# The S5 generator of a four-branch mixer begins among the gate tiles, with longer pairs of steps

## The chip, the cores and the metric

The kernel runs on one core of one Trainium2 chip. The core's engines work side by side, each from its own queue in order: TensorE (PE, with its weight loads apart as PEld), VectorE (DVE), ScalarE (ACT), GpSimd (POOL), and SyncE (SP), which issues DMA transfers. The metric is the device time of one execution in microseconds (us).

## The reference, cut to what matters

Two layers, each over 256 context tokens and 1024 latent tokens of width 1024. One projection of the normed input feeds four mixers (latent attention, a diagonal S5 state space model, a gated linear recurrence, pooling), four gate paths and four sets of merge logits:

```python
def _merge(branches, gate_paths, merge_logits, w_branch, w_out):
    gp = jnp.split(gate_paths, N_BRANCH, axis=-1)
    ml = jnp.split(merge_logits, N_BRANCH, axis=-1)
    y = 0.0
    for n in range(N_BRANCH):
        y = y + jax.nn.sigmoid(ml[n]) * ((branches[n] * jax.nn.silu(gp[n])) @ w_branch[n])
    return y @ w_out
```

The S5 mixer has 16 groups with 64 complex states each, run over the tokens forwards and backwards; a readout gives back 16 channels per group, and a GLU with one 256x256 product follows.

In the first layer all 1280 tokens are produced, in the second the context is only read, so its output covers the 1024 latent tokens.

## The kernel before

Activations lie channels by tokens. The tokens are cut in three chunks, `CH = [(0, 256), (256, 512), (768, 512)]`; the first layer (0) works on all three where it makes outputs, the second (1) on the last two. A projection tile is one 128-column slice of `w_in`: `load_w` fetches it (`wr`) and splits it in a high and a low part (`wh` on ACT, `wl` on DVE, line 117), and `hgemm` runs 24 matmuls for each chunk into a PSUM tile `pg`, which has two buffers.

After the attention, `layer` issues in this order of the program: the six gate tiles that the pooling has left over (`gate`: three chunks each in layer 0, two in layer 1), the eight logit tiles of the pooling branch (`logits`), and `merge`, which goes through the branches in the order pooling, recurrence, attention, S5. The merge of the pooling branch is short: 6 matmuls `pm<-b,wph/wpl` for each tile and chunk, and one DVE instruction `y<-y,pm` that takes the result, since its logits are there already. The `pm` tiles have two buffers. The later branches compute their logit tile (24 matmuls) ahead of each such product.

The S5 work between them is a Python generator, `s5`, of eight pairs of groups. A pair first forms its matrices on DVE (`tm<-hao`, `er<-tm`, `wc<-tm`, `ph<-tm`), transposes them on PE (`pS<-ident,er`), then makes its state products (`pS<-u,wb`, copied to `rqx`), rotates them (`tm<-rqx,ph`, `er<-tm`), scans them (eight scans, lines 935 and 936, `rqx<-hkeep,er`), rotates back into `er`, and reads out on PE (`pS<-u,wk` and `pS<-er,wc`, copied to `yo`, stored to `yD`). The generator stops at `yield`:

```python
for _ in range(lead[0]):   # ahead of the state products
    yield
...
for _ in range(lead[1]):   # from the rotation back to the readout
    yield
...
yield                      # behind the readout
```

and after the pairs `s5_out` adds two stops for each chunk ahead of its GLU product (`pS<-rqx,er`). Each chunk of a logit tile calls `next(s5)` once, and so does each chunk of a merge tile of the second and third branch (`if bi > 0: ... next(s5, None)`); before the S5 branch's merge, `for _ in s5: pass` runs what is left.

The order of the program is not the order on the engines. A scheduler takes instructions by priority (their place in the program, earlier first, with `hp()` blocks put ahead) as soon as its own estimate says that their inputs are there, and writes one fixed order for each engine. So gate tiles fill the attention's gaps on PE, and the S5 pairs are taken up when the attention leaves PSUM (`pS`, three buffers shared) and DVE to them.

Of the kernel before, what the change touches and what calls it, by code (L numbers as in the profile page):

```python
# [36 lines left out]
MLA, S5B, LRUB, POOLB = 0, 1, 2, 3  # L37
# [26 lines left out]
class Net:  # L64
# [928 lines left out]
                self.dma(oD[f][:, s0:s0 + n], t)  # L993


    def gate(self, l, b, f, lat, gD):

        w = self.load_w(self.I["w_in"][l, 9 + 2 * b + f], NK)
        for ci in lat:
            s0, n = CH[ci]  # L1000
            ps = self.hgemm(w, ci)
            t = self.st(n)
            with self.hp():
                self.act(t, ps, AF.Tanh, scale=0.5)
                self.stt(t, t, 1.0, ps, ALU.add, ALU.mult)
                self.dma(gD[f][:, s0:s0 + n], t)

    def logits(self, l, b, j, lat, tD, bg):

        w = self.load_w(self.I["w_in"][l, 17 + 8 * b + j], NK)  # L1010
        for ci in lat:
            s0, n = CH[ci]
            ps = self.hgemm(w, ci)
            t = self.st(n)
            with self.hp():
                self.act(t, ps, AF.Tanh, scale=0.5)
                self.dma(tD[j][:, s0:s0 + n], t)
            next(bg, None)
# [105 lines left out]
    def layer(self, l, pre):  # L1124
        tc = self.tc
        lat = [0, 1, 2] if l < DEPTH - 1 else [1, 2]
        oD = {b: self.dram((2, 128, NT), "oD") for b in ORDER}
        gD = {b: self.dram((2, 128, NT), "gD") for b in ORDER}
        with self.phase("pr") as pr, self.phase("pa") as pa:
            m = self.mla_in(l, pa, pre)  # L1130
            pads = [self.lru_pad(pa, pre[2 + f]) for f in range(2)] if pre else None
            self.mla_kv(l, m, pa)
            uF, uD = self.s5_in(l, pr)
            xl = self.lru_in(l, pa, pads)
            self.lru(l, xl, oD[LRUB], lat, pa, pr)
            self.cq_in(l, m, lat, pa)
            self.mla_q(l, m, lat, pa)
            xp = self.pool_in(l, lat, pa)
            gates = ((b, f) for b in ORDER for f in range(2))
            for _ in self.pool(l, xp, oD[POOLB], lat, pa, pr):  # L1140
                b, f = next(gates)
                self.gate(l, b, f, lat, gD[b])
        with self.phase("p5") as p5:
            with self.phase("pt") as pt_:
                self.attention(m, lat, oD[MLA], pt_)
            for b, f in gates:
                self.gate(l, b, f, lat, gD[b])
            s5 = self.s5(l, uF, uD, oD[S5B], lat, p5, (2, 4) if len(lat) == 3 else (1, 3))
            tD = self.dram((NK, 128, NT), "tD")
            for j in range(NK):  # L1150
                self.logits(l, ORDER[0], j, lat, tD, s5)
            with self.phase("pc") as pc:
                self.merge(l, lat, oD, gD, tD, pc, s5)
# [269 lines left out]
```

## Time and profile before

| what | us |
|---|---|
| median of 3 runs (2327.64 to 2333.63) | 2330.84 |
| the profiled execution | 2328.08 |
| its span in the trace | 2326.3 |
| PE busy in it | 2267.7 |
| DVE busy in it | 1547.8 |
| ACT busy in it | 969.2 |

PE is the engine that counts: it has work nearly all the time. Its busy time takes in matmuls that overlap, so what it loses is read from its idle time in the waits and the timeline, and from the pace of matmuls (24 of a chunk in 5.6 us), not from the busy share. DVE's share is a mean over stages in which it is loaded very differently.

### The profile page before, as it was taken

Reading aid. Unit: us, or ns where it says so; the run is one execution under the profiler, and the core shown is the slowest. Engines: PE = TensorE matmul, PEld = TensorE weight load, DVE = VectorE, ACT = ScalarE, POOL = GpSimd, SP = SyncE. Lnnn points to the kernel's source line nnn. Section 1 sums busy time; section 2 is a strip of 40 time slices with the busy share of each in tenths; the row PEclk is TensorE's granted clock in tenths of the full one; section 3 lists DMA queues with packets and bytes.
Section 4 is the critical chain, followed back from the end, with each engine's and each line's share of the span. In section 5 each row is a group of like instructions: output and inputs, shape, how many; then the busy total and the mean of one; then the engine's idle time right before and its main releaser. Section 6 shows DMA issues by size and latency. Waiting matters only on the chain. (4 is left out here: it accounts for less than half of the span.)

```text
span 2326.3 us, 33035 instructions
## 1 busy us (share of the span) xinstructions
PE 2267.7 (97%) x11680; PEld 1848.0 (79%) x11680; DVE 1547.8 (67%) x3524; ACT 969.2 (42%) x1966; POOL 208.3 (9%) x261
## 2 busy tenths in 40 slices
PE   8899999999999999999999999999999999999999
PEld 3687878888788888788888787778888788877887
DVE  5664769676877888656455745688667978863243
ACT  4646656665312222312243445756664232322131
POOL 0000000000001111111112100000000011111100
PEclk9999999999999999999999999999999999999999
DMA  8141242211534223433234332242213431332134
GB/s 278 56 157 40 103 123 67 76 56 54 174 94 122 74 77 109 127 94 104 96 100 157 115 116 70 99 132 73 70 56 116 118 105 53 86 110 85 49 115 157
DMA packets 215750, 236.34 MB, mean 102 GB/s; under 512 B 78112, under 2 KB 141344, under 8 KB 215584
## 3 DMA queue, kind: packets, MB, share of 16 engines
q1 hardware_dynamic: 215072, 234.19, 32.4%
q8 instruction: 92, 1.51, 0.3%
q0 software_dynamic: 512, 0.03, 0.1%
q14 instruction: 74, 0.61, 0.1%
HBM read 175.70 MB, written 58.46 MB: 101 GB/s over the span
## 5 line engine op out<-in xcount | busy, mean ns | idle before, releaser
L135 PE MATMUL pg<-h,wh 128*128 128x512 f32 (+1 forms) x4608 | 1346.8, 374 | 0.2 <-DVE h L117 0.2
L135 PEld LDWEIGHTS pg<-h,wh 128*128 128x128 f32 x4608 | 828.7, 188 | 154.6 <-issue 4.5
L135 PE MATMUL pg<-h,wl 128*128 128x512 f32 (+2 forms) x2304 | 871.1, 378 | 1.8 <-DVE wl L117 1.6
L135 PEld LDWEIGHTS pg<-h,wl 128*128 128x128 f32 (+1 forms) x2304 | 434.0, 188 | 81.1 <-issue 3.6
L117 DVE TENSOR_TENSOR wl<-wr,wh 128x512 fp32r<-128x512 f32 x268 | 190.3, 712 | 172.0 <-ACT wh L132 171.1
L132 ACT ACTIVATE wh<-wr 128x512 fp32r<-128x512 f32 x268 | 167.9, 628 | 277.9 <-PE pg L135 150.8
L132 ACT ACTIVATE st<-pg 128x512 f32<-128x512 f32 (+1 forms) x200 | 110.4, 552 | 350.5 <-PE pg L135 343.1
L117 POOL TENSOR_TENSOR y<-y,st 128x512 f32<-128x512 f32 (+1 forms) x120 | 153.1, 1276 | 733.8 <-DVE st L120 696.3
L135 PE MATMUL pm<-b,wph 128*128 128x512 f32 (+1 forms) x640 | 184.4, 372 | 1.6 <-DVE b L117 1.6
L132 ACT ACTIVATE P<-pS,sm,qs 128x512 f32<-128x512 f32 (+1 forms) x200 | 138.6, 702 | 45.3 <-DVE sm L124 43.2
L135 PE MATMUL pS<-k,q 128*128 128x512 f32 (+1 forms) x600 | 145.4, 365 | 0.6 <-DVE q L117 0.4
L120 DVE SCALAR_TENSOR_TENSOR st<-st,pm 128x512 f32<-128x512 f32 (+1 forms) x120 | 75.5, 629 | 105.4 <-PE pm L135 104.9
L135 PEld LDWEIGHTS pm<-b,wph 128*128 128x128 f32 x640 | 115.7, 188 | 24.5 <-DVE b L117 3.1
L135 PE MATMUL pP<-pt,v 128*128 128x256 f32 x656 | 126.9, 301 | 3.4 <-DVE pt L117 1.2
L135 PEld LDWEIGHTS pP<-pt,v 128*128 128x128 f32 x656 | 99.1, 188 | 35.1 <-ACT pt L132 21.5
L117 DVE TENSOR_TENSOR pt<-pm,pt 128x512 fp32r<-128x512 f32 x164 | 107.0, 683 | 26.5 <-ACT pt L132 25.8
L135 PE MATMUL pm<-b,wpl 128*128 128x256 f32 (+1 forms) x320 | 120.1, 376 | 4.5 <-ACT b L132 2.6
L518 DVE TENSOR_REDUCE sm<-pS 128x1 f32<-128x512 f32 (+1 forms) x200 | 113.4, 587 | 14.3 <-PE pS L135 13.0
L132 ACT ACTIVATE pt<-pm 128x512 fp32r<-128x512 f32 x164 | 91.0, 600 | 70.5 <-PE pm L138 70.1
L135 PEld LDWEIGHTS pS<-k,q 128*128 128x128 f32 x600 | 98.7, 189 | 18.6 <-ACT P L132 4.8
L138 PE MATMUL pm<-ident,P 128*128 128x128 f32 x656 | 106.3, 274 | 0.2 <-ACT P L132 0.2
L120 DVE SCALAR_TENSOR_TENSOR pP<-wa,cv,pP 128x256 f32<-128x256 f32 x196 | 95.3, 486 | 13.9 <-DMA wa<-in_w_ada 10.1
(243 smaller groups left out, 2508.0 us busy)
## 6 DMA issues: line engine op xcount, KB each, us to landing
wr<-in_w_in SPq DMA_DIRECT2D x196, 256.0 KB, 2.7
wa<-in_w_ada SPq DMA_DIRECT2D x96, 256.0 KB, 2.9
wr<-in_w_out SPq DMA_DIRECT2D x64, 256.0 KB, 2.8
gD<-st SPq DMA_DIRECT2D x32, 256.0 KB, 2.0
tD<-st SPq DMA_DIRECT2D x32, 256.0 KB, 2.2
og<-oD SPq DMA_DIRECT2D x32, 256.0 KB, 2.7
og<-gD SPq DMA_DIRECT2D x32, 256.0 KB, 3.0
wr<-in_w_branch SPq DMA_DIRECT2D x64, 128.0 KB, 2.1
```

The lines of the kernel that those rows point to most:

```text
L117: (eng or self.nc.vector).tensor_tensor(out=out, in0=a, in1=b, op=op)
L120: self.nc.vector.scalar_tensor_tensor(out=out, in0=a, scalar=s, in1=b, op0=op0, op1=op1)
L132: self.nc.scalar.activation(out=out, in_=a, func=func, scale=scale, **kw)
L135: self.nc.tensor.matmul(out=out, lhsT=lhsT, rhs=rhs, start=start, stop=stop)
L138: self.nc.tensor.transpose(out=out, in_=in_, identity=ident)
L518: nc.vector.tensor_reduce(out=mx3[:, i:i + 1], in_=S, axis=AX.X, op=ALU.max)
```

## The change

The generator is made ahead of the gate tiles, each chunk of a gate tile calls `next` on it, and `lead` goes from (2, 4) to (2, 6) in layer 0 and from (1, 3) to (2, 4) in layer 1.

```diff
-    def gate(self, l, b, f, lat, gD):
+    def gate(self, l, b, f, lat, gD, bg=iter(())):
...
                 self.dma(gD[f][:, s0:s0 + n], t)
+            next(bg, None)
...
+            s5 = self.s5(l, uF, uD, oD[S5B], lat, p5, (2, 6) if len(lat) == 3 else (2, 4))
             for b, f in gates:
-                self.gate(l, b, f, lat, gD[b])
-            s5 = self.s5(l, uF, uD, oD[S5B], lat, p5, (2, 4) if len(lat) == 3 else (1, 3))
+                self.gate(l, b, f, lat, gD[b], s5)
```

No instruction is added or taken away. On PE the order is the same through the first pair's readout in layer 0, and again in layer 1 from the start of its attention until just ahead of the third pair's readout. Three places where it moves follow; the numbers in names are of the scheduler's own and differ between the two kernels.

DVE in layer 0, the fourth pair's scans (`rqx<-hkeep,er`). Before, among the sums of the pooling branch's merge (`y<-y,pm`):

```order
L935 SCALAR_TENSOR_TENSOR rqx_6822<-hkeep_5553,er_6831 64x192
L117 TENSOR_TENSOR er_6831<-tm_6723 128x384
L120 SCALAR_TENSOR_TENSOR y_6864<-y_6864,pm_6960 128x512
L936 SCALAR_TENSOR_TENSOR rqx_6822<-hkeep_5553,er_6831 64x192
L935 SCALAR_TENSOR_TENSOR rqx_6822<-hkeep_5553,er_6831 64x192
L120 SCALAR_TENSOR_TENSOR y_6864<-y_6864,pm_6968 128x512
L120 SCALAR_TENSOR_TENSOR y_6865<-y_6865,pm_6983 128x256
L117 TENSOR_TENSOR wpl_7010<-wr_7008,wph_7009 128x256
L936 SCALAR_TENSOR_TENSOR rqx_6822<-hkeep_5553,er_6831 64x192
L935 SCALAR_TENSOR_TENSOR rqx_6822<-hkeep_5553,er_6831 64x192
L936 SCALAR_TENSOR_TENSOR rqx_6822<-hkeep_5553,er_6831 64x192
```

Now:

```order
L117 TENSOR_TENSOR er_6447<-tm_6339 128x384
L117 TENSOR_TENSOR wpl_7028<-wr_7026,wph_7027 128x256
L935 SCALAR_TENSOR_TENSOR rqx_6438<-hkeep_4959,er_6447 64x192
L936 SCALAR_TENSOR_TENSOR rqx_6438<-hkeep_4959,er_6447 64x192
L935 SCALAR_TENSOR_TENSOR rqx_6438<-hkeep_4959,er_6447 64x192
L936 SCALAR_TENSOR_TENSOR rqx_6438<-hkeep_4959,er_6447 64x192
L935 SCALAR_TENSOR_TENSOR rqx_6438<-hkeep_4959,er_6447 64x192
L936 SCALAR_TENSOR_TENSOR rqx_6438<-hkeep_4959,er_6447 64x192
L935 SCALAR_TENSOR_TENSOR rqx_6438<-hkeep_4959,er_6447 64x192
L936 SCALAR_TENSOR_TENSOR rqx_6438<-hkeep_4959,er_6447 64x192
```

The fourth pair's scans have gone ahead of the merge's sums; beside them stands only a weight part (`wpl`) that the merge will use.

DVE in layer 1, the pooling branch's merge (`y<-y,pm`, with the low parts `wpl` of its weights). Before, with the forming of the fourth pair's `ph` (`y<-cm` is S5's own small tile):

```order
L120 SCALAR_TENSOR_TENSOR y_17880<-y_17880,pm_17932 128x512
L117 TENSOR_TENSOR wpl_17966<-wr_17964,wph_17965 128x256
L117 TENSOR_TENSOR ph_17870<-tm_17834 128x384
L120 SCALAR_TENSOR_TENSOR y_17881<-y_17881,pm_17947 128x512
L117 TENSOR_TENSOR tm_17834<-hun_16920 128x384 x2
L120 SCALAR_TENSOR_TENSOR y_17881<-y_17881,pm_17955 128x512
L117 TENSOR_TENSOR wpl_17989<-wr_17987,wph_17988 128x256
L120 SCALAR_TENSOR_TENSOR y_17882<-y_17882,pm_17970 128x512
L117 TENSOR_TENSOR ph_17870<-tm_17834 128x384
L117 TENSOR_TENSOR y_18411<-cm_18407,hkeep_16850 128x32 x2
L120 SCALAR_TENSOR_TENSOR y_17882<-y_17882,pm_17978 128x512
L117 TENSOR_TENSOR wpl_18012<-wr_18010,wph_18011 128x256
```

Now:

```order
L117 TENSOR_TENSOR tm_17630<-rqx_17741,ph_17666 128x384
L120 SCALAR_TENSOR_TENSOR y_17927<-y_17927,pm_18037 128x512
L117 TENSOR_TENSOR er_17750<-tm_17630 128x384
L120 SCALAR_TENSOR_TENSOR y_17927<-y_17927,pm_18045 128x512
L117 TENSOR_TENSOR wpl_18079<-wr_18077,wph_18078 128x256
L935 SCALAR_TENSOR_TENSOR rqx_17741<-hkeep_16430,er_17750 64x192
L936 SCALAR_TENSOR_TENSOR rqx_17741<-hkeep_16430,er_17750 64x192
L120 SCALAR_TENSOR_TENSOR y_17928<-y_17928,pm_18060 128x512
L935 SCALAR_TENSOR_TENSOR rqx_17741<-hkeep_16430,er_17750 64x192
L936 SCALAR_TENSOR_TENSOR rqx_17741<-hkeep_16430,er_17750 64x192
L120 SCALAR_TENSOR_TENSOR y_17928<-y_17928,pm_18068 128x512
```

The fourth pair's rotation (`tm<-rqx`, `er<-tm`) and its scans have come up into the merge; before they stood behind it.

PE in layer 1, the last GLU product of the S5 branch (`pS<-rqx,er`), for the last chunk. Before, behind a merge product of the attention branch:

```order
L135 MATMUL pm_19988<-b_17888,wpl_19957 128x512
L135 MATMUL pm_19988<-b_17888,wph_19956 128x512 x2
L135 MATMUL pm_19988<-b_17888,wpl_19957 128x512
L135 MATMUL pm_19988<-b_17888,wph_19956 128x512 x2
L135 MATMUL pS_19997<-rqx_19884,er_19755 128x512 x2
L135 MATMUL pS_20004<-rqx_19884,er_19755 128x512 x2
L135 MATMUL pg_20011<-h_84,wl_19945 128x512
L135 MATMUL pg_20011<-h_84,wh_19944 128x512 x2
```

Now, inside the first logit tile of the S5 branch's merge (`pg` with the new number; the other two of these four products stand 15 rows ahead, behind the end of the attention branch's last tile):

```order
L135 MATMUL pg_20183<-h_84,wh_20172 128x512 x2
L135 MATMUL pg_20183<-h_84,wl_20173 128x512
L135 MATMUL pg_20183<-h_84,wh_20172 128x512
L135 MATMUL pS_20123<-rqx_20064,er_19935 128x512
L135 MATMUL pS_20130<-rqx_20064,er_19935 128x512
L135 MATMUL pg_20183<-h_84,wh_20172 128x512
L135 MATMUL pg_20183<-h_84,wl_20173 128x512
L135 MATMUL pg_20183<-h_84,wh_20172 128x512 x2
L135 MATMUL pm_20210<-b_17932,wpl_20179 128x512
L135 MATMUL pm_20210<-b_17932,wph_20178 128x512 x2
L135 MATMUL pm_20210<-b_17932,wpl_20179 128x512
```

The last chunk's GLU products have gone from three merge tiles ahead of the S5 branch's own merge to the first tile of it.

## Rows read from the trace of the kernel before

**Rows 1.** The page: span; busy us (share) and instructions of each engine.

```profile
span 2326.3 us, 33035 instructions
PE 2267.7 (97%) x11680; PEld 1848.0 (79%) x11680; DVE 1547.8 (67%) x3524; ACT 969.2 (42%) x1966; POOL 208.3 (9%) x261
```

**Rows 2.** Waits of PE, longest first: us in total, times, longest us.

```profile
PE pS L135 <- DVE er L117: 11.2, 6, 2.6
```

**Rows 3.** Timeline of PE: start, us, instruction, [idle before <- releaser]; the S5 readouts.

```profile
584.69 0.81 PE L135 MATMUL pS<-er,wc 128*128 128x160 f32 x4 [1.93 <-DVE er L117]
...
618.41 0.54 PE L135 MATMUL pS<-er,wc 128*128 128x160 f32 x2 [1.91 <-DVE er L117]
...
1788.67 1.22 PE L135 MATMUL pS<-er,wc 128*128 128x128 f32 x4 [2.22 <-DVE er L117]
...
1811.63 0.71 PE L135 MATMUL pS<-u,wk 128*128 128x128 f32 x4 [0.62 <-ACT wk L132]
1818.92 1.08 PE L135 MATMUL pS<-er,wc 128*128 128x128 f32 x4 [2.61 <-DVE er L117]
...
1841.44 0.71 PE L135 MATMUL pS<-er,wc 128*128 128x128 f32 x4 [2.23 <-DVE er L117]
```

**Rows 4.** Stretches: length, busy of PE, PEld, DVE, ACT, POOL; granted clock, DMA.

```profile
870.00:892.00 22.00, 19.60 (x91) 15.63 (x90) 20.59 (x43) 7.96 (x20) 3.95 (x4) 0.92 0.59 167
...
1792.00:1822.00 30.00, 26.76 (x123) 21.39 (x123) 26.89 (x62) 9.27 (x22) 0.76 (x1) 0.95 0.65 192
1822.00:1844.00 22.00, 19.67 (x99) 15.97 (x98) 19.94 (x49) 5.67 (x14) 0.76 (x1) 0.99 0.30 86
...
1902.00:1941.00 39.00, 39.00 (x185) 32.22 (x184) 30.40 (x61) 10.07 (x24) 7.86 (x6) 1.00 0.21 63
```

**Rows 5.** Timeline of DVE: the last write of er ahead of a readout.

```profile
586.77 0.56 DVE L117 TENSOR_TENSOR er<-tm 64x256 f32<-64x256 f32 x2
...
617.31 1.05 DVE L117 TENSOR_TENSOR er<-tm 64x318 f32<-64x318 f32 x3
...
1790.50 0.91 DVE L117 TENSOR_TENSOR er<-tm 64x318 f32<-64x318 f32 x2
...
1820.57 0.91 DVE L117 TENSOR_TENSOR er<-tm 64x318 f32<-64x318 f32 x2
1823.60 0.17 DVE L854 MEMSET er<- 128x128 f32 x1 [1.33 <-PE pS L135]
...
1842.67 0.92 DVE L117 TENSOR_TENSOR er<-tm 64x318 f32<-64x318 f32 x2
```

**Rows 6.** Chain that ended last, around one paced pair: start us, us, what.

```profile
1901.30 1.34 PE pS L135 x12
1902.64 5.59 PE pg L135 x24
...
1910.06 0.81 PE pS L135 x8
...
1917.96 1.30 PE pS L135 x8
```

**Rows 7.** Timeline of PE: waits behind the first pairs.

```profile
688.29 0.50 PE L135 MATMUL pm<-b,wpl 128*128 128x512 f32 x1 [0.80 <-DVE y L120]
...
722.70 0.50 PE L135 MATMUL pm<-b,wpl 128*128 128x512 f32 x1 [0.72 <-ACT b L132]
...
877.50 0.74 PE L135 MATMUL pm<-b,wph 128*128 128x512 f32 x2 [0.76 <-DVE b L117]
879.68 0.55 PE L138 MATMUL pS<-ident,er 128*128 128x128 f32 x3 [1.33 <-DVE er L117]
...
1886.60 0.72 PE L135 MATMUL pm<-b,wph 128*128 128x512 f32 x2 [0.51 <-DVE b L117]
```

**Rows 8.** Chain and DVE timeline, the last two GLU products of layer 1.

```profile
2079.19 3.43 PE pS L135 x8
...
2095.91 0.69 DVE L120 SCALAR_TENSOR_TENSOR rqx<-wb,rqx 128x512 f32<-128x512 f32 x1 [0.70 <-ACT wb L132]
```

## The prediction

> **What bounds the kernel now.** I read the page's first part, then who TensorE (PE) waits for, then the timeline of those waits, then single stretches.
>
> PE is busy for 97% of the span and VectorE (DVE) for 67% [rows 1]: the time is the matmuls' own plus what PE waits. The change touches S5, and S5 has the longest entry among PE's waits: PE stood six times, 11.2 us in all, for DVE's `er`, the input of a readout [rows 2]. The timeline says where: at the first and second pair of layer 0 (1.93 and 1.91) and at the first three pairs of layer 1 (2.22, 2.61 and 2.23, and 0.62 for `wk`) [rows 3]; these five make 10.9 of the 11.2. So no readout of a later pair was waited for. Around the early ones DVE is full, with 26.89 us of 30 and 19.94 of 22; in a stretch with a late pair PE loses nothing and DVE works 30.40 of 39 [rows 4]. The early pairs of each layer are thus bound by DVE, all else here by PE.
>
> The pace of DVE is read from the last write of `er` of one pair to that of the next [rows 5]. Layer 1, first to second pair: 1791.41 to 1821.48, 30.1 us; second to third: to 1843.59, 22.1 us. The order of DVE has 12 instructions that are not S5's (weight splits, `og`, `b`) in the first interval and none in the second. So a pair is 22.1, and another instruction (30.1 - 22.1) / 12 = 0.66. Layer 0, first to second pair: 587.33 to 618.36, 31.0 with 13 others, so a pair is 31.0 - 13 x 0.66 = 22.4. Of PE: 24 matmuls of 512 columns take 5.59, 0.233 each, half of that for 256; S5's own in a pair 1.34 + 0.81 + 1.30 = 3.45 [rows 6], in layer 0 some 3.8 with its wider readouts. The two paces explain the waits: second to third pair of layer 1, 62 matmuls are 14.4 + 3.45 = 17.9 against DVE's 22.1, 4.2 short; PE waited 2.23 there, and a granted clock of 0.95 in the 30 us around it [rows 4], half speed for a tenth of them, accounts for 1.5 more.
>
> **The change part by part.** *More steps.* They put the readout later in the program, and that helps only where PE waits at a readout. In layer 1 PE's order is the same until just before the third readout, in layer 0 through the first: five of the six long waits stand where they stood. Only layer 0's second (1.91) can change. Pairs that go by the steps waited for none, so more steps give nothing there.
>
> *The earlier start.* It doesn't move the first pair either, which still comes when the attention leaves. It changes how many pairs are due by then. By the end of the logit tiles layer 0 has made 24 calls of 7 a pair, 3.4 pairs; now 18 + 24 of 9, 4.7. Layer 1: 16 of 5, 3.2; now 28 of 7, 4.0. So in each layer one pair more is taken up as fast as the scheduler believes it can be, in the stretch that DVE already binds.
>
> *Layer 0, first to fourth readout.* The new order has between them 69 + 54 + 55 matmuls `pg` of 512 columns and 48 + 24 + 24 of 256: 41.5 + 11.2, and 3 x 3.8 of S5, 64.1 us of PE. DVE has three pairs and 14 + 2 + 4 other instructions: 67.3 + 13.2 = 80.5. PE is short of 16.4. Before, the same PE work cost only the 1.91: the second to third interval had 120 + 48 `pg`, 37.4 against DVE's 22.4 + 6 x 0.66 = 26.4, and the third to fourth was mixed with the pooling merge. Cost: 16.4 - 1.9 = 14.5.
>
> *Layer 1, third to fourth readout.* The fourth pair now lies in the pooling merge: 122 matmuls, 28.4 + 3.45 = 31.9 of PE, against a pair and 27 other instructions of DVE (16 `y`, 7 of the half-size `wpl`, 4 more), 22.1 + 27 x 0.66 = 39.9. That is 8.0 at the high end. The low end takes the mean over all DVE instructions of a full stretch, 26.89 / 62 = 0.43, and the pair without its own idle 1.33 [rows 5]: 20.8 + 11.6 = 32.4, 0.5. I take 4.4, between them, since a quarter of the 27 are half-size.
>
> *What comes back.* The work that DVE has done earlier is not in its way later. Behind the first pairs PE waited in layer 0 three times for `y` (0.36, 0.52 and 0.80; the last is shown), three times for ACT's `b` (0.66, 0.72, 0.56; the middle one is shown), and at the eighth pair 0.76 and 1.33 [rows 7], with the clock at 0.92 in the 22 us around, 1.8 us of PE [rows 4], and 0.31 more: 7.7 in all. In layer 1 twice, 0.63 and 0.51 (shown), 1.1. The fourth pair no longer shares the pooling merge of layer 0, and the eighth is formed before the branch changes, so I give back the `y` waits and the eighth pair's whole, 1.7 + 2.1 + 1.8 = 5.6, and half of the other 3.3: 7.2.
>
> *The end of layer 1.* S5 needs 60 calls and gets 12 + 16 + 32 = 60, so the last GLU falls to the loop that drains the generator, ahead of the S5 branch's merge; before, 44 of 48. The last input of that GLU was written 14.0 us after the first GLU's products had ended (2082.62 to 2096.60) [rows 8]. PE now has 30 matmuls, two GLU products and 20 matmuls in between, 7.0 + 1.7 + 4.7 = 13.4: 0.6 of wait. The branch's `og` and `b` for the last chunk are late too; PE has its other chunk and two logit tiles there, which I let hide them. If they are not hidden, I bound it by the longest wait of rows 2, 2.6.
>
> *The rest costs nothing.* The same DMAs go through SP's queue, S5's loads for a pair ahead of some logit stores and of a merge load; POOL's accumulating DMAs for `s5g` come earlier, ahead of the merge's sums, on an engine that is busy for 9% [rows 1]. ACT has 9.27 of 30 in the full stretch [rows 4]. If a weight's load is late behind them, DVE's split of it is late as well; in the DVE-bound stretch that adds to the same wait.
>
> Sum: 14.5 + 4.4 + 0.6 - 7.2 = +12.3 on the profiled 2328.08, 2340.4. The median of the runs stands 2.8 above that execution, so 2343.
>
> Low end: a pair of 20.8 and others of 0.43 make 71.0 in layer 0, 6.9 short, 5.0 more than before; all 7.7 comes back; layer 1 gives 0.5 - 1.1: -3, 2328. High end: nothing comes back, 14.5 + 8.0 + 0.6 + 2.6 = 25.7: 2356.
>
> **A page that would add to it.** In the trace the clock fell from 2.4 to 1.2 GHz behind waits of 2.2 and 2.6 us in layer 1 (0.95 in 1792 to 1822), yet after the wait of 2.23 it stood at 0.99 [rows 4]. The Trainium skill, "TensorE: Matmul & The Clock Gate", Part 1, has the array fall to half clock when it has been idle and rise again when busy; by that, each new wait takes its own toll. In rows, a toll is 1.5 us, and four new waits make 6: 2349, if PE binds right after them. But it is DVE that binds there, and a slow PE eats only its own next wait, as the 17.9 + 1.5 + 2.2 against 22.1 above shows. I hold this as a rival.
>
> **The rivals.**
> - *The waits go, faster.* The six waits and the clock's 1.5 in layer 1 vanish: 12.7 off, 2318. For it: the change lengthens just the way from the rotation to the readout. Against it: five readouts keep their place. It is decided where PE's work between two readouts exceeds DVE's 22; the order has 19.4 or less after the second and the third. 0.06.
> - *All of it comes back, no change.* The price of DVE at its low end and every later wait gone: 2328 to 2336. For it: DVE has the same work in total, and 33% of the span free. Against it: PE waits for `y` and `b` also where DVE is not full. 0.24.
> - *The clock on top.* 2349, as above. 0.12.
> - *The drain shows.* The last GLU's inputs are only begun once the first GLU has freed `rqx`; were none of the 7.0 us of the tile ahead of it a cover, PE would wait 7 more: 2350. 0.05.
>
> **How the numbers follow.** The forecast, 2343, has 0.53, and its own range is 2337 to 2350. A measurement can't tell less than 0.3%, 7 us, from no change, so slower begins at 2338. Slower takes the forecast but its low edge, the clock and the drain: 0.69. Same takes the case without change and that edge: 0.25. Faster 0.06. The range for eight in ten goes from 2330 to 2354: it leaves out the faster case and the far ends.
>
> **What would show it.** Right: in layer 0 PE waits of 2 to 6 us at the second, third and fourth readout, DVE full (over 85%) for some 80 us from the first to the fourth, no long wait at the eighth pair's transposes; in layer 1 the first three waits as now, and PE stretched in the pooling merge by some us. Wrong: `er` waits fewer than six or below 11 us, or a DVE that idles between the first four readouts of layer 0; and if layer 0 as a whole loses no time, what comes back is larger than I put it.

## The result, and the profile after

The changed kernel took 2346.8 us (median of 4, 2342.94 to 2352.88) beside 2329.5 for the kernel before on the same chip (median of 4): a ratio of 1.0076, with a 95% interval of 1.0062 to 1.0090, so 14 to 21 us slower. The forecast was 2343, its range 2330 to 2354. The profiled execution of the changed kernel took 2342.94, 14.9 more than that of before.

The page's engine rows (as [rows 1]), then the longest S5 and merge entries among PE's waits (as [rows 2]):

```profile
span 2341.2 us, 33026 instructions
PE 2271.5 (97%) x11680; PEld 1848.3 (79%) x11680; DVE 1547.1 (66%) x3524; ACT 972.6 (42%) x1966; POOL 207.4 (9%) x261
```

```profile
PE pS L135 <- DVE er L117: 13.4, 7, 2.4
...
PE pm L135 <- ACT b L132: 7.3, 5, 3.5
...
PE pS L135 <- DVE rqx L120: 4.0, 3, 2.5
PE pS L135 <- DVE er L947: 2.7, 1, 2.7
```

All the work is the same; PE waits more. With the row that names line 947 (one of the small memsets in the same tile) the readouts now cost 16.1 us in eight waits, where [rows 2] had 11.2 in six. The waits for `b`, the gated branch output that a merge multiplies, have grown from 2.6 to 7.3. The timeline of PE says where (as [rows 3], [rows 7] and [rows 8]):

```profile
584.47 0.81 PE L135 MATMUL pS<-er,wc 128*128 128x160 f32 x4 [1.93 <-DVE er L117]
...
614.97 1.40 PE L135 MATMUL pS<-er,wc 128*128 128x160 f32 x4 [2.73 <-DVE er L947]
...
638.95 1.44 PE L135 MATMUL pS<-er,wc 128*128 128x160 f32 x4 [2.39 <-DVE er L117]
...
663.22 0.81 PE L135 MATMUL pS<-er,wc 128*128 128x160 f32 x4 [2.11 <-DVE er L117]
...
897.93 0.50 PE L135 MATMUL pm<-b,wpl 128*128 128x512 f32 x1 [3.50 <-ACT b L132]
...
954.59 1.98 PE L135 MATMUL pS<-rqx,er 128*128 128x512 f32 x4 [2.45 <-DVE rqx L120]
...
1826.13 0.71 PE L135 MATMUL pS<-er,wc 128*128 128x128 f32 x4 [2.27 <-DVE er L117]
...
1848.64 0.71 PE L135 MATMUL pS<-er,wc 128*128 128x128 f32 x4 [2.24 <-DVE er L117]
...
2136.75 1.98 PE L135 MATMUL pS<-rqx,er 128*128 128x512 f32 x4 [1.35 <-DVE rqx L120]
...
2152.97 0.50 PE L135 MATMUL pm<-b,wpl 128*128 128x512 f32 x1 [1.45 <-ACT b L132]
```

In layer 0 the third and fourth readout have joined the first two; in layer 1 the first three stand as before. New are a wait for `b` where layer 0 changes branch (897.93), one at its first GLU (954.59, on the GLU's input `rqx`; it was 0.22 before), and two at the end of layer 1. The waits at the eighth pair ([rows 7]: 1.33 at its transposes, 0.76 for `b`) are gone.

The stretches (as [rows 4]): the first four readouts of layer 0, two around the end of the recurrence branch, the second to the third readout of layer 1, and its pooling merge.

```profile
584.00:670.00 86.00, 77.45 (x407) 65.16 (x408) 80.26 (x208) 27.82 (x68) 2.27 (x3) 0.96 0.49 145
870.00:892.00 22.00, 22.00 (x118) 18.80 (x116) 17.31 (x34) 7.19 (x13) 4.62 (x3) 1.00 0.47 133
890.00:905.00 15.00, 11.50 (x58) 9.73 (x57) 13.90 (x28) 3.76 (x7) 2.69 (x3) 0.89 0.30 98
1822.00:1844.00 22.00, 19.73 (x93) 16.05 (x93) 20.01 (x50) 5.49 (x14) 0.76 (x1) 0.92 0.39 115
1851.00:1885.00 34.00, 31.89 (x146) 24.87 (x147) 31.72 (x67) 9.12 (x22) 0.76 (x1) 1.00 0.29 84
```

In the kernel before, the first of these stretches reads:

```profile
584.00:670.00 86.00, 83.13 (x449) 71.03 (x450) 65.74 (x170) 25.75 (x61) 2.27 (x3) 1.00 0.52 157
```

So DVE is now busy for 93% of the 86 us instead of 76%, and PE for 77.45 us instead of 83.13. The other stretches hold different work in the two kernels, since the program has shifted, and are not to be compared by their start times.

To compare stages I also worked out from each trace what PE loses: for each matmul the distance to the start of the next, less what that distance usually is for the same form in the kernel before (its 20th percentile). That takes in waits, small gaps and half-speed matmuls. A layer begins here 8 us ahead of its first readout, and its stages end with the last merge product of each branch:

| lost by PE, us | L0 pooling | L0 rest | L1 pooling | L1 2nd, 3rd | L1 4th |
|---|---|---|---|---|---|
| before | 9.7 | 19.1 | 13.3 | 4.2 | 1.1 |
| changed | 17.3 | 19.9 | 15.1 | 5.3 | 4.5 |
| difference | +7.6 | +0.8 | +1.8 | +1.1 | +3.4 |

These five differences make 14.7 of the 14.9 by which the two spans differ. One execution is loose by some us here: the order of layer 0 was traced four times as changed (17.1 to 18.9 in the pooling stage, 19.9 to 25.5 in the rest) and twice as before (9.7 and 12.2; 19.1 and 21.5), over the runs below.

### The profile page after: what moved, and what is told of

Read it like the earlier page. It is cut to its first block, busy times and chain, and to the rows that moved or that the text cites. A ratio compares the mean times of both kernels' runs of the same rounds, so it can differ in the third digit from the quotient of the medians.

```text
span 2341.2 us, 33026 instructions
## 1 busy us (share of the span) xinstructions
PE 2271.5 (97%) x11680; PEld 1848.3 (79%) x11680; DVE 1547.1 (66%) x3524; ACT 972.6 (42%) x1966; POOL 207.4 (9%) x261
## 4 chain that ended last, share of the span: by engine, by line
PE 48%; DVE 6%; ACT 2%; DMA 2%; issue 1%; POOL 0%; SPq 0%; ACTq 0%; DVEq 0%; POOLq 0%
PE pg L135 33%; PE pm L135 6%; PE pS L135 5%; PE pP L135 3%; PE pm L138 1%; DVE st L120 1%; DVE tm L117 1%; DVE wl L117 1%; DVE h L120 1%; DMA s5g<-y 1%; DMA og<-gD 0%; DVE rqx L936 0%; DVE er L117 0%; ACT pt L132 0%; PE pS L138 0%
## 5 line engine op out<-in xcount | busy, mean ns | idle before, releaser
L135 PEld LDWEIGHTS pP<-pt,v 128*128 128x128 f32 x656 | 99.1, 188 | 35.0 <-ACT pt L132 21.5
L518 DVE TENSOR_REDUCE sm<-pS 128x1 f32<-128x512 f32 (+1 forms) x200 | 113.2, 586 | 14.8 <-PE pS L135 13.6
```

What stands on the lines that cost most here:

```text
L135: self.nc.tensor.matmul(out=out, lhsT=lhsT, rhs=rhs, start=start, stop=stop)
L518: nc.vector.tensor_reduce(out=mx3[:, i:i + 1], in_=S, axis=AX.X, op=ALU.max)
```

## The experiments

Every time is given by its ratio to the kernel before, run beside it on one chip (median 2331 to 2334 there).

**Start alone.** The generator begins among the gate tiles, the steps are the old ones.

```diff
-            s5 = self.s5(l, uF, uD, oD[S5B], lat, p5, (2, 6) if len(lat) == 3 else (2, 4))
+            s5 = self.s5(l, uF, uD, oD[S5B], lat, p5, (2, 4) if len(lat) == 3 else (1, 3))
```

> The earlier start alone, with a pair's steps as before (2 and 4, 1 and 3). Theory (VectorE's pace: each pair that is due while VectorE is full costs TensorE some 4 to 5 us, whatever the number of steps): with short steps five pairs of layer 0 and all eight of layer 1 are due early, so there are more waits at readouts than in the changed kernel (10 or more of about 2 us), partly given back later; slower than the changed kernel, 2348 to 2362. Rival (the longer steps and what they push to the end make the loss): without them no more than before, 2326 to 2334. Rival (all of it comes back): S5 is only done sooner, 2328 to 2336.

2371.9 us, 1.0158 (1.0133 to 1.0184): 37 us slower, beyond the top of the range I had given the theory, and twice the loss of the whole change. PE's wait entry for `er`, and three of the rows in layer 1's second branch:

```profile
PE pS L135 <- DVE er L117: 29.1, 13, 4.2
```

```profile
1922.99 0.71 PE L135 MATMUL pS<-er,wc 128*128 128x128 f32 x4 [3.47 <-DVE er L117]
...
1952.68 1.22 PE L135 MATMUL pS<-er,wc 128*128 128x128 f32 x4 [4.24 <-DVE er L117]
...
1980.38 1.22 PE L135 MATMUL pS<-er,wc 128*128 128x128 f32 x4 [4.10 <-DVE er L117]
```

The more pairs are due early, the more readouts wait (13 in that entry, instead of 7 in the changed kernel). PE loses 24.1 in layer 0's pooling stage (17.3 in the changed kernel, 9.7 before), 16.3 in layer 1's and 26.0 in its second branch; the ends of both layers are as short as before (1.1 in layer 1's fourth branch). Both rivals fall. It also tells what the longer steps are worth beside this start: 37 - 18 = 19 us.

**Steps alone.** Old start, new steps, so the calls don't suffice.

```diff
-            s5 = self.s5(l, uF, uD, oD[S5B], lat, p5, (2, 4) if len(lat) == 3 else (1, 3))
+            s5 = self.s5(l, uF, uD, oD[S5B], lat, p5, (2, 6) if len(lat) == 3 else (2, 4))
```

> The longer steps alone, with the generator started where it was, so 78 calls of layer 0 meet 72 stops and 60 of layer 1 meet 48, and the rest is drained ahead of the last branch. Theory (VectorE's pace; the start decides which pairs are early): the readouts behind the first of layer 0 are no longer waited for, 2 us, and in layer 1 two of three, some 5; against that the last pairs' readouts and GLUs fall to the drain with waits there; early waits under 6 us in all, total 2326 to 2345, the loss if any in the last 100 us of each layer's S5. Rival (longer steps are what costs): waits at the early readouts as long as in the changed kernel, 13 us, total 2340 or more without a wait in the drain. Rival (longer steps are the gain, as meant): 2318 to 2322.

2363.6, 1.0128 (1.0107 to 1.0149): 30 us slower, outside the theory's range and for the reason it named last. The early stages get better, 4.4 lost instead of 9.7 in layer 0 and 3.9 instead of 13.3 in layer 1, with no wait at any early readout but the first of each layer. The drain, the loop that runs what is left ahead of the last branch, takes it back threefold: 23.8 instead of 5.6 in the stage of layer 0's last branch, 29.4 instead of 1.1 in layer 1's. Its rows there are GLU products that wait for their own input, and a logit tile that cannot leave PSUM since ACT's `st` is behind:

```profile
2163.70 2.93 PE L135 MATMUL pS<-rqx,er 128*128 128x512 f32 x3 [5.96 <-DVE rqx L120]
...
2171.70 2.93 PE L135 MATMUL pS<-rqx,er 128*128 128x512 f32 x3 [3.67 <-DVE rqx L120]
...
2179.59 0.50 PE L135 MATMUL pg<-h,wl 128*128 128x512 f32 x1 [2.82 <-ACT st L132]
```

So longer steps do remove early waits, 14.7 us of them, as long as the start is the old one; what they cost is the drain.

**Layer 0 alone, layer 1 alone.** The call in the gate tiles and the new steps in one layer, the old in the other.

```diff
+                self.gate(l, b, f, lat, gD[b], *([s5] if l == 0 else []))
```

> The whole change in layer 0 alone. Theory (the fourth pair of each layer at VectorE's pace): layer 0 ends some 8 us later than before and layer 1 takes as long as before: 2336 to 2341. Rival (what the changed kernel loses lies at the end of layer 1, in the drain): 2328 to 2333.

> The whole change in layer 1 alone. Theory (the fourth pair at VectorE's pace, some 4 us in the pooling merge, and the last GLU behind the drain, 2 to 3 us): 2334 to 2339, the half of the loss that layer 0 alone doesn't have. Rival (layer 1 only shows what layer 0 has shifted): 2328 to 2333.

Layer 0 alone: 1.0036 (1.0024 to 1.0049), 8.4 us. Layer 1 alone: 1.0016 (1.0004 to 1.0028), 3.7. Layer 0 is as the theory said, and in its trace layer 1 loses 17.1 as before (18.6). Layer 1 alone came out at the low end of its range, and its runs had a slightly higher granted clock than those of the kernel before beside them (0.9933 and 0.9925 on the mean); its trace has the same lengthening of layer 1 as the changed kernel's, 450.7 us from the first readout to the last merge product where the kernel before takes 443.5 and the changed one 449.8. The profiled execution was a long one of its kind (span 2344.2, where the median of its runs is 2337.9), with 5 us more lost in layer 0, whose order is that of before.

**Both again.** The changed kernel once more.

> The changed kernel as it is, beside the others on one chip, since layer 0 alone came to +8.4 and layer 1 alone to +3.7 of before, 12.1 together, where the changed kernel had 17.3 in its own measurement. Theory (the layers add up, VectorE's pace in each by itself): 10 to 14 us above before here. Rival (something that needs both layers' changes): 16 or more above before.

1.0079 (1.0064 to 1.0093), 18.4 us. The two layers alone make 12.1, with an interval of some 4 either way. The stage table has no part that needs both layers, but the sum by the ratios stays 6 short of the whole. About 4 of the 6 go with the granted clock, by an estimate from all runs. Over the 23 runs of the kernel before that stand beside the two single layers, the span grows by 1.7 us for each 0.001 that the mean granted clock is lower (2.0 over the 17 beside "both again"). That clock was 0.0010 lower with layer 0 alone than in the kernel before, 0.0008 higher with layer 1 alone, and 0.0024 lower with both: 1.7 - 1.4 us for the two layers, 4.1 for the whole. The other 2 us are within the intervals.

**ph on GpSimd, before and changed.** The six instructions of a pair that form `ph` go to GpSimd, with their scratch in the tile `rqx`.

```diff
-            self.tt(m1, coarse(0), fine(0), ALU.mult)
+            self.tt(g1, coarse(0), fine(0), ALU.mult, nc.gpsimd)
...
```

> The kernel before, with the six instructions that form ph on GpSimd instead of VectorE, so some 3 us less of VectorE's work in each pair (19 instead of 22). Theory (VectorE's pace at the early pairs): of the five early readout waits, 10.9 us, half goes, in 5 intervals up to 2.5 each; 2322 to 2328. Rival (a chain that is as long on any engine, or GpSimd is the slower one): the readouts are waited for as long or longer, now behind GpSimd, 2330 or more.

> The changed kernel with the six ph instructions on GpSimd. Theory (its loss is VectorE's pace at three pairs of layer 0 and one more of layer 1): 7 readouts gain up to 2.5 us each, 8 to 14 us faster than the changed kernel, and 5 to 12 us above the kernel before with the same edit instead of 12 to 17. Rival (the loss is the end of layer 1 and the clock): the distance between the two stays at 12 to 17 us.

The kernel before became slower by 1.0083 (1.0068 to 1.0098), the changed one stands at 1.0227 (1.0206 to 1.0248) of the unaltered kernel before: their distance is 34 us. So the second expectation missed on both sides: the changed kernel got slower by some 34 us too, and the distance grew. As a test of VectorE's load this failed, since it did not unload VectorE. The timeline of the first:

```profile
1800.42 0.91 DVE L117 TENSOR_TENSOR er<-tm 64x318 f32<-64x318 f32 x2
...
1802.65 2.22 POOL L117 TENSOR_TENSOR rqx<-hun 128x384 f32<-128x384 f32 x2 [15.09 <-DVE tm L117]
1803.01 2.14 DVE L117 TENSOR_TENSOR er<-tm 64x318 f32<-64x318 f32 x2
1804.94 1.06 POOL L117 TENSOR_TENSOR ph<-rqx 128x384 f32<-128x384 f32 x1
1805.18 1.37 DVE L117 TENSOR_TENSOR wl<-wr,wh 128x512 fp32r<-128x512 f32 x1
...
1806.48 1.35 DVE L117 TENSOR_TENSOR b<-og,b 128x512 fp32r<-128x512 f32 x1
```

The same two `er` instructions take DVE 0.91 us alone and 2.14 beside GpSimd, a `wl` 1.37 where it is 0.68 alone. And `ph` can only begin when the pair before has left `rqx` (the releaser in the first POOL row). So the rival "GpSimd is the slower one" holds, with causes that this run doesn't part: its own 1.05 us per instruction, VectorE's doubled ones beside it, the later start, and a lower granted clock (0.9906 on the mean, beside 0.9927).

**Less for VectorE, before and changed.** Left out: `ph` is formed for the first pair only, and four of the eight scans are not run. Nothing goes to another engine.

```diff
+            if q == 0:
                 self.tt(m1, coarse(0), fine(0), ALU.mult)
...
-            for k in range(2):
+            for k in range(1):
```

> The kernel before with less of VectorE's work in S5 and no other engine given more: ph is formed for the first pair only, and the second half of the state is not scanned (four of eight scans left out), some 5.5 us less in a pair, 16.6 instead of 22.1. The scheduler knows that these are gone and sets the readouts closer, so not all of it shows. Theory (VectorE's pace at the early pairs): the readout waits fall from 11 us to 5 to 8; 3 to 8 us faster than before, 2326 to 2331. Rival (these waits are a fixed delay between VectorE and TensorE, not its load): the same waits of about 2 us at as many readouts, no more than 2 us faster.

> The changed kernel with the same work left out (ph for the first pair only, four of eight scans). Theory (the loss is VectorE's pace at the early pairs, of which the change has one more in each layer): 8 to 14 us faster than the changed kernel, and the distance to the kernel before with the same work left out shrinks from 17 to 5 to 12. Rival (the order alone makes the loss, whatever VectorE has to do): the distance stays at 15 to 19.

Before: 0.9939 (0.9923 to 0.9955), 14 us faster, more than I expected; PE's `er` entry falls from 11.2 us to 1.1. Changed: 0.9987 (0.9975 to 0.9999), which is 21 us below the changed kernel. The distance shrinks from 18 us to 11, with some 4 us either way on each. The stretch that answers to the changed kernel's first, and its longest S5 waits:

```profile
584.00:670.00 86.00, 81.81 (x451) 70.61 (x452) 67.14 (x184) 29.62 (x73) 3.03 (x4) 0.98 0.54 151
```

```profile
PE pS L135 <- ACT wk L132: 6.7, 4, 2.1
PE pm L135 <- ACT b L132: 6.0, 6, 2.5
...
PE pS L135 <- DVE rqx L120: 4.1, 2, 2.7
```

With VectorE at 78% instead of 93% the entry `er` is gone from the top (2.3 us instead of 13.4); a second chain shows in its place, `wk`, which goes out to DRAM and comes back by a DMA before ACT copies it. In the kernel before, the same edit left PE losing 4.6 in layer 0's pooling stage and 5.4 in layer 1's, instead of 9.7 and 13.3. So VectorE's time is what those waits are made of. The edit takes instructions out of a pair's chain and out of VectorE's load at once, and the scheduler writes a new order for it, so whether the load or the length of the chain counts is not parted here. Part of the distance remains (9.9 against 4.6 in layer 0's pooling stage); that the next chain then binds, since the pairs are so near to one another, fits the `wk` rows but is not shown.

**Spread.** Old start, and one step more from the rotation to the readout only where the calls allow it.

```diff
-            for _ in range(lead[1]):
+            for _ in range(lead[1] + (len(lat) == 2 and q < 3)):
...
-            s5 = self.s5(l, uF, uD, oD[S5B], lat, p5, (2, 4) if len(lat) == 3 else (1, 3))
+            s5 = self.s5(l, uF, uD, oD[S5B], lat, p5, (2, 5) if len(lat) == 3 else (1, 3))
```

> The generator starts where it did before the change, and a pair has one step more from the rotation to the readout: every pair of layer 0 (2 and 5) and the first three of layer 1, so that 70 of 72 and 47 of 48 calls are used and nothing falls to the drain. Theory (what costs is only that pairs are due closer to one another than VectorE's 22 us; the first readout of a layer waits anyway): the second and third waits of layer 1, 4.8 us, its clock toll of 1.5, and the second of layer 0, 1.9, go, and nothing comes in their place: 5 to 9 us below before, 2322 to 2329. Rival (the waits come at the place where a pair is taken up, not from its distance to the next): they move with the readouts, 2329 to 2335. Rival (later pairs crowd the branch changes): a new wait there of 3 us or more for b or og takes it back, 2329 to 2336.

0.9959 (0.9947 to 0.9972): 9.6 us faster than the kernel before, so it beats both kernels with all of the work done. The same stretch of layer 0, and what is left of the early waits in layer 1:

```profile
584.00:670.00 86.00, 83.93 (x446) 71.38 (x445) 59.69 (x151) 23.80 (x53) 1.52 (x2) 1.00 0.53 156
```

```profile
1783.71 1.22 PE L135 MATMUL pS<-er,wc 128*128 128x128 f32 x4 [2.21 <-DVE er L117]
...
1814.13 1.22 PE L135 MATMUL pS<-er,wc 128*128 128x128 f32 x4 [2.46 <-DVE er L117]
```

Layer 0's pooling stage loses 4.7 instead of 9.7. In layer 1 the third wait is gone and the second is not (10.4 lost instead of 13.3), and what the pooling stage gained there is lost again behind it, 7.8 instead of 5.3. So by the stage table nearly all of the gain, 8.0 of 8.4 us, lies in layer 0 (20.8 lost instead of 28.8), while the expectation had put most of it in layer 1: the total came out at the top of its 5 to 9 us, but not by its terms.

**Spread, more.** In layer 1 four steps more for the second pair alone, one less for the last; in layer 0 one less for the last two.

```diff
-            for _ in range(lead[1] + (len(lat) == 2 and q < 3)):
+            for _ in range(lead[1] + ((0, 4, 0, 0, 0, 0, 0, -1)[q] if len(lat) == 2 else (0, 0, 0, 0, 0, 0, -1, -1)[q])):
```

> As the spread version that came out faster (start as before the change), but in layer 1 the second pair alone has four more steps and the last one less (47 of 48 calls), and in layer 0 the last two pairs are one step shorter (68 of 72). On TensorE 30.8 us instead of 24.0 now lie between the first two readouts of layer 1, by the order. Theory (a readout waits only where TensorE's work between two is less than VectorE's): the 2.46 there, 0.95 for wk and the clock's toll of 1.5 go, and the 1.75 at the GLU of layer 0: 3 to 6 us below the spread version, 11 to 16 below before, 2317 to 2322. Rival (the gain of the spread version was in layer 0 alone, or such waits come back at once in the next stage): within 2 us of the spread version, 2322 to 2326.

0.9968 (0.9956 to 0.9981), 7.5 us faster than the kernel before: the rival, no better than the spread version. The second wait is gone and layer 1's pooling stage loses 6.7 instead of 10.4, but the branches behind it lose 9.8 instead of 7.8; one of the waits there:

```profile
2069.82 0.49 PE L135 MATMUL pS<-er,wc 128*128 128x128 f32 x2 [1.52 <-DVE er L117]
```

**Last pair shorter.** The changed kernel, 59 stops for the 60 calls of layer 1.

```diff
-            for _ in range(lead[1]):
+            for _ in range(lead[1] - (len(lat) == 2 and q == 7)):
```

> The changed kernel with the last pair of layer 1 one step shorter, 59 stops for 60 calls, so that the last GLU comes one chunk earlier and is not in the drain. Theory (the drain's GLU has no cover for its last input and delays the branch's b): the waits of 1.35 at that GLU and 1.45 for b behind it go, 2 to 4 us of the 118.5 between the end of the third and of the last branch's merge; total 0 to 4 us below the changed kernel. Rival (the last stage is longer only because the GLU's products moved into it): the stage keeps its length but for the 3.6 us of one GLU, and the third branch takes these; the same total.

1.0070 (1.0052 to 1.0088), beside 1.0079 for the changed kernel: 2 us, within the noise of both. The stage shows it: from the third to the last branch's end 116.0 us instead of 118.5, lost 2.0 instead of 4.5, and the third branch takes 121.7 in both. The drain's GLU without cover cost 2.5.

## Why the prediction came out

The direction was right, and so was the cause, pairs of S5 that are due at VectorE's pace. That the total came so near (12.3 us forecast, 14.9 in the profiled pair, 17.7 by the ratio) is luck: the first term was some 7 us too high, and of the 7.2 us that were to come back nothing was left. By its own steps:

- **More steps: "more steps give nothing there"** was wrong as put. Where they move the readout they take waits away: 14.7 us with the old start, some 19 us of what the new start would cost. It is right only that in the changed kernel, with the earlier start, layer 1's first three stand where they stood; with the old start the second and third of them went.
- **The earlier start makes one pair more due in each layer, which then runs at VectorE's pace**: right. In layer 0 the first to the fourth readout took 663.22 - 584.47 = 78.7 us (80.5 forecast), with VectorE at 93%; start alone, spread and less for VectorE all move the loss the way of this step.
- **Layer 0, +14.5**: the price of the new order was about right, 13.6 lost between these readouts against 16.4. What failed is the subtraction: "before, the same PE work cost only the 1.91". From its first to its fourth readout the kernel before lost 6.8 us, of which the 1.9 is one wait; 1.7 are the `y` waits, which I counted in the next step, and the rest lies in pieces under 0.5 us that the list of waits doesn't single out. The term measured is 6.8 to 7.6.
- **Layer 1, +4.4**: its pooling stage lost 1.8 more in the profiled pair, and over all traces of the two orders 15.9 on the mean (four traces) instead of 12.6 (two), so about 3. The profiled pair shows less because the kernel before had one stretch at half clock more there; see the clock below.
- **What comes back, -7.2**: the step that failed. It came to +0.8 in the rest of layer 0 and +1.1 in layer 1's second and third branch. The eighth pair's waits did go; its transposes now start at 861.77 with no wait. But the eighth pair's scans now lie where the attention branch's first products need `b`. DVE there, in the changed kernel:

```profile
888.43 0.68 DVE L120 SCALAR_TENSOR_TENSOR og<-og,og 128x512 f32<-128x512 f32 x1
889.03 0.54 DVE L935 TENSOR_TENSOR_SCAN rqx<-hkeep,er 64x192 f32<-64x192 f32 x1
...
895.47 0.56 DVE L936 TENSOR_TENSOR_SCAN rqx<-hkeep,er 64x192 f32<-64x192 f32 x1
...
896.53 0.68 DVE L120 SCALAR_TENSOR_TENSOR og<-og,og 128x512 f32<-128x512 f32 x1
```

  Between two `og` of the branch lie 8 scans and other work; PE waits 3.50 for the `b` made from the second (3.46 to 3.51 in the three other traces of this order), and the stretch 890 to 905 has clock 0.89. With the 2.45 at layer 0's first GLU that is more than the 2.1 that went.
- **The end of layer 1, +0.6** (bounded at +2.6 more, 3.2): 3.4, just above the bound. The GLU waited 1.35, and the branch's `b` was not hidden, 1.45. Making the last pair one step shorter gave back 2.5.
- **The rivals.** "The waits go" and "All of it comes back" fell with the result. "The drain shows" put 7 us where 3.4 were.
- **"The clock on top"** was set aside with "it is DVE that binds there, and a slow PE eats only its own next wait". That step failed. From the first to the second readout of layer 1 the order of PE and of DVE is the same in both kernels, and DVE has the same work. These are the two intervals from the first to the third readout, in the kernel before and then in the changed one, as [rows 4]:

```profile
1788.67:1818.92 30.25, 27.01 (x122) 21.65 (x122) 27.14 (x61) 9.90 (x23) 0.76 (x1) 0.95 0.70 211
1818.92:1841.44 22.52, 20.29 (x94) 16.71 (x94) 20.49 (x52) 5.67 (x14) 0.76 (x1) 0.92 0.35 102
```

```profile
1797.28:1826.13 28.85, 25.85 (x122) 20.40 (x123) 27.16 (x61) 9.91 (x23) 0.76 (x1) 1.00 0.72 218
1826.13:1848.64 22.51, 20.27 (x94) 16.49 (x95) 20.49 (x52) 5.67 (x14) 0.76 (x1) 0.92 0.35 102
```

  Before, the clock fell to its lower level at the first readout's wait; in the changed kernel's trace it did not, and the interval is 1.4 us shorter, though the second readout waits in both (2.61 and 2.27). Five more traces have the same order there: 30.40, 30.22 and 29.98 us at clock 0.94 (both again, start alone, layer 1 alone), 28.82 and 29.07 at 1.00 (layer 0 alone, last pair shorter). So a slow PE costs 0.9 to 1.6 us here too. DVE shows the way, at the first write of the next pair into `er`, before and changed:

```profile
1793.44 0.17 DVE L854 MEMSET er<- 128x128 f32 x1 [1.23 <-PE pS L135]
```

```profile
1800.89 0.17 DVE L854 MEMSET er<- 128x128 f32 x1
```

  DVE waits until PE has read `er`, so a readout at half clock holds up the engine that sets the pace. In the second interval both kernels had the same clock, 0.92, and the same time. ([rows 4] cut one slow stretch in two at 1822, hence the 0.95 and 0.99 there.) In layer 0 the changed kernel's second to third readout took 23.98 us at 0.93, and 23.02 at 0.99 when it was run again. For the whole kernel, the 1.7 us for each 0.001 of mean clock, from above, give the clock some 4 of the 18.4 us of "both again", an estimate, where the rival put 6; the sum had it at nothing. The clock falls at waits, so this part is not independent of the order; at which of them it falls differs between runs of one kernel.

Not settled: how much of the loss that is left with a light VectorE is `wk`'s way through DRAM. PE's waits for it are 6.7 us in the changed kernel with less for VectorE and 1.9 in the kernel before with the same edit, but no run took that way out. Nor did a run give `er` a second buffer.

## What to carry to other kernels

When background work is made in slices between the steps of a main loop, count how many of its units are due inside the stretch where the helping engine is already full, and compare the main engine's work between two units with the helper's time for one. That told the sign here, and spreading the units over the calls that were there was what gained. Starting such work earlier did not help, since the stretch it started in was bound by the engine that does it. And a wait that goes away is not time given back until one has looked at what the moved work is now queued ahead of: here eight scans came to stand before the one product that a branch change waits for.

## What the runs showed of the hardware

Beside GpSimd's two-input fp32 instructions VectorE's own took about twice as long (2.14 instead of 0.91 us for two of 64x318, 1.37 instead of 0.68 for one of 128x512). The Trainium skill, "SBUF — State Buffer", section "SBUF: two separate sides", has the two engines share a port pair that one instruction holds to its end, where VectorE reads two inputs from SBUF and GpSimd reads SBUF too; the rows of the GpSimd run agree, with 2.14 us for VectorE's two beside 2.22 for GpSimd's two. For the 128x384 product from `hun` GpSimd took 1.05 us on the mean, VectorE in the kernel before 0.62. So moving such work to the engine that is busy for 9% made the kernel 19 us slower.

A stretch of TensorE at its lower clock level, 1.2 GHz, cost 0.9 to 1.6 us also where VectorE was busy for some 90% and set the pace (30.25 and 28.85 us for the same order, at 0.95 and 1.00), because VectorE could not write `er` again before the slowed readout had read it.
